# Another order at two joints of a transformer block, and POOL's sums queued behind each other

## The chip, the cores and the metric

The kernel runs on one core of a Trainium2 chip. The metric is the device time of one launch in microseconds (us), the median over the runs shown. A profiled execution comes with it: one launch recorded by the hardware profiler, with the start and length of every instruction of the engines: PE (TensorE's matmuls), PEld (its weight loads), DVE (VectorE), ACT (ScalarE), POOL (GpSimd, here a queue of adding DMAs) and SP (SyncE, here the queue of weight loads).

## The reference, cut to what matters

One block on 512 tokens of width 1024, all in float32:

```
x = x + 0.5 * swiglu(rmsnorm(x), ffn1_w_gu, ffn1_w_down)      # FFN 1, hidden width 2816
x = x + hybrid_mixer(rmsnorm(x), w_in, ..., w_out_conv, w_out_gla, w_o)
x = x + 0.5 * swiglu(rmsnorm(x), ffn2_w_gu, ffn2_w_down)      # FFN 2
return rmsnorm(x)
swiglu(x, w_gu, w_down) = (silu(x @ w_gu[:, :2816]) * (x @ w_gu[:, 2816:])) @ w_down
hybrid_mixer(h, ...)    = (sigmoid(ga) * y_conv + sigmoid(gb) * y_gla) @ w_o
```

`ga`, `gb` and what `y_conv` and `y_gla` are made of are columns of `h @ w_in`; `y_conv` ends in a product with `w_out_conv`, `y_gla` in one with `w_out_gla`.

## The kernel before, in words

**Seven products instead of eight.** Most of the large matrix products are computed by halves of the weight block in both directions (quarters a11, a12, a21, a22), with seven products in place of eight (Strassen-Winograd). Such a group of seven is called a *set*. Its products are named by the weights they use: `m1` (a11), `p2` (a12), `q6` (a11 after a21 has been added to it), `p5` (a21 after a22 has been added to it), `q7` (s3 = a11 + a21, taken before the additions), `p4` (a22), `p3` (a12 after a11 has been added to it).

**Where a product goes.** Each set has three PSUM banks. `m1` opens bank b, from which ACT copies it to bank a; `q6`, `q7` and `p4` are accumulated onto b, `p2` onto a, and `p5` opens c, onto which `p3` is accumulated. Between two products onto bank b the first has to be copied out, or read, by ACT or DVE; the next one cannot start before that.

**Weights.** float32 weights come from HBM by SP's queue (`Weights.dma`, line 349) into ten slots of 512 KB (tiles `f`). The sums among the quarters are DMAs that add, issued on POOL's queue (`Weights.add`, line 376): the *first sum* of a set (a21 += a22), the add of `m1` (a11 += a21) and the add of `p2` (a12 += a11). `s3` is a DVE addition (line 387). Each product's weight is then split into a high part `wh` (a cast on ACT, line 407) and a low part `wl` (a subtraction on DVE, line 408), three buffers of each; the product is wh with the high and the low part of the activations, then wl with the high part. A product with 256-wide matmuls follows the next after 2.88 us.

**The order of the work.** `STEPS` is the list of all products in order, written out by rules: `order` for the sets of `w_gu` ("up sets") and `w_in`, the list `LAST_SEQ` for four sets at the end of the mixer (sets 0 and 1 are `w_out_gla`, 2 and 3 are `w_o`), `wide_sets` for the down products. `Weights.take` hands out the next split weight and issues the work of the steps up to two ahead. `Weights.phase` says at which step a set's loads and its first sum are issued. A scheduler at compile time then fixes each engine's order from the dependencies, the order of the program and its own model of time; on the chip each engine and each queue works through its list in order. `tc.issue_after(ins)` adds a tie: what is issued inside it *on the engine of `ins`* is queued behind `ins`; on other engines it ties nothing.

**The first joint: up sets to down.** In each FFN nine up sets are followed by the two down products. The last up set, here called set 8, is *narrow* (256-wide matmuls, line 566); sets 1 to 7 are wide (line 575). The down product is *lean*: to save slots, its first sum adds a22 straight from HBM onto a21 (`f<-wts` on POOL in the trace), in three pieces, and its products come as `m1` three times, `p5` three times, `q6` three times and so on (line 874).

**The second joint: the end of the mixer.** The operands of the `w_o` sets are made from the outputs of the `w_out_gla` sets, in place, in the order given to `Operands` (`mo`). Their outputs are the new rows of x; when a pair of rows is complete, `NORMS` says where its part of the next RMSNorm is issued (ACT lines 492 to 501, DVE lines 493 and 502).

## Time and profile before

| what | before |
|---|---|
| median of 3 runs (lowest, highest) | 1166.3 us (1165.94, 1167.74) |
| the profiled execution: time; span of its instructions | 1167.14 us; 1165.4 us |
| PE busy, share of the span | 1147.3 us, 98% |
| DVE busy | 994.7 us, 85% |
| ACT busy | 710.0 us, 61% |
| POOL busy | 134.7 us, 12% |
| mean granted TensorE clock | 0.996 |

PE works nearly all the time, so what can be won by order alone is what PE does not work: read first where PE is idle and what ended the wait, then whether the clock was full when it started again. In the views below a row of the timeline gives start, length, engine, line, operation, tiles out<-in, shapes, how many instructions were merged and, in brackets, the idle time before it and what ended that. PE tiles x, y, z, w are the banks of the up sets, `mm` and `aux` those of the others.

### The profile page before, as it was taken

The numbers are of one execution on the slowest core, as the hardware profiler recorded it, in microseconds if no ns is written. First come the engines' busy times: TensorE is split into PE (matmuls) and PEld (weight loads), VectorE is DVE, ScalarE is ACT, GpSimd is POOL, SyncE is SP. The second block draws the span as 40 slices with busy tenths as digits, with TensorE's granted clock in tenths as the row PEclk, the third lists the DMA queues.
The fourth block names the chain that finished last, engine by engine and source line by source line (L and its number), as shares of the span: only waits on it lengthen the run. The fifth ranks groups of instructions, "written<-read, shape, count | busy, mean of one in ns | idle before, by whom it ended". The sixth has DMA issues, their size and how long they took to land. (4 is left out here: it accounts for less than half of the span.)

```text
span 1165.4 us, 17576 instructions
## 1 busy us (share of the span) xinstructions
PE 1147.3 (98%) x6734; PEld 1017.7 (87%) x6734; DVE 994.7 (85%) x1248; ACT 710.0 (61%) x958; POOL 134.7 (12%) x171
## 2 busy tenths in 40 slices
PE   9999999899999999999999999999999999989997
PEld 8898888788888889999989998999889888888886
DVE  7997878779788977979799998699799887888987
ACT  6476666567355655666566586555556666655645
POOL 0011101011020011100101100110001111111100
PEclk9999999999999999999999999999999999999999
DMA  9378787769564488876868867575637878776941
GB/s 354 80 205 201 179 196 178 181 136 255 143 198 134 98 205 232 197 177 172 228 170 210 210 170 216 131 177 150 184 77 199 195 186 183 185 183 138 246 109 73
DMA packets 65764, 208.01 MB, mean 178 GB/s; under 512 B 7216, under 2 KB 13488, under 8 KB 65680
## 3 DMA queue, kind: packets, MB, share of 16 engines
q0 software_dynamic: 21376, 76.03, 35.4%
q1 hardware_dynamic: 39664, 126.37, 32.4%
q10 hardware_dynamic: 4640, 4.49, 1.2%
q8 instruction: 53, 0.87, 0.3%
q14 instruction: 31, 0.25, 0.1%
HBM read 130.32 MB, written 8.39 MB: 119 GB/s over the span
## 5 line engine op out<-in xcount | busy, mean ns | idle before, releaser
L407 ACT CAST wh<-f 128x1024 fp32r<-128x1024 f32 (+1 forms) x366 | 375.6, 1031 | 365.7 <-PE mm L874 41.8
L408 DVE TENSOR_TENSOR wl<-f,wh 128x1024 fp32r<-128x1024 f32 (+1 forms) x366 | 435.9, 1197 | 95.4 <-ACT wh L407 88.7
L376 POOL DMA_DIRECT2D f<-f x132 | 114.7, 871 | 850.4 <-DVE wl L408 545.2
L874 PE MATMUL mm<-wh,op 128*128 128x512 f32 x536 | 133.7, 389 | 0.0
L566 PE MATMUL mm<-op,wh 128*128 128x256 f32 x960 | 127.2, 284 | 0.5 <-ACT op L678 0.4
L566 PEld LDWEIGHTS mm<-op,wh 128*128 128x128 f32 x960 | 120.2, 192 | 1.5 <-ACT op L678 0.6
L874 PEld LDWEIGHTS mm<-wh,op 128*128 128x128 f32 x536 | 100.4, 188 | 20.7
L575 PE MATMUL bb<-op,wh 128*128 128x512 f32 x384 | 97.8, 395 | 0.0
L575 PEld LDWEIGHTS bb<-op,wh 128*128 128x128 f32 x384 | 69.4, 189 | 12.6
L442 PE MATMUL mm<-op,wh 128*128 128x512 f32 x320 | 75.8, 389 | 0.0
L874 PE MATMUL mm<-wl,op 128*128 128x512 f32 x268 | 72.8, 389 | 0.0
L442 PEld LDWEIGHTS mm<-op,wh 128*128 128x128 f32 x320 | 60.0, 188 | 12.5
L566 PE MATMUL mm<-op,wl 128*128 128x256 f32 x480 | 67.8, 283 | 0.0
L575 PE MATMUL z<-op,wh 128*128 128x512 f32 x256 | 64.4, 393 | 0.0
L566 PEld LDWEIGHTS mm<-op,wl 128*128 128x128 f32 x480 | 62.1, 192 | 0.3
L874 PEld LDWEIGHTS mm<-wl,op 128*128 128x128 f32 x268 | 50.3, 188 | 10.5
L575 PEld LDWEIGHTS bb<-op,wl 128*128 128x128 f32 x384 | 52.3, 190 | 5.0 <-DVE wl L408 1.3
L575 PE MATMUL w<-op,wh 128*128 128x512 f32 x224 | 56.3, 393 | 0.0
L575 PE MATMUL bb<-op,wl 128*128 128x256 f32 x384 | 53.6, 282 | 0.9 <-DVE wl L408 0.9
L575 PEld LDWEIGHTS z<-op,wh 128*128 128x128 f32 x256 | 46.0, 189 | 8.3
L779 DVE TENSOR_TENSOR op<-hidw,op 128x1024 fp32r<-128x1024 f32 (+2 forms) x56 | 48.6, 885 | 0.7 <-ACT op L778 0.7
L456 PE MATMUL mm<-op,wh 128*128 128x512 f32 x192 | 48.4, 392 | 0.0
(334 smaller groups left out, 1954.5 us busy)
## 6 DMA issues: line engine op xcount, KB each, us to landing
f<-wts SPq DMA_DIRECT2D x215, 512.0 KB, 4.4
f<-f POOLq DMA_DIRECT2D x128, 512.0 KB, 5.3
f<-wts POOLq DMA_DIRECT2D x10, 512.0 KB, 8.6
f<-wts SPq DMA_DIRECT2D x10, 256.0 KB, 3.5
X<-xT SPq DMA_DIRECT2D x8, 256.0 KB, 4.7
xs<-X POOLq DMA_DIRECT2D x8, 256.0 KB, 3.1
tp<-ga SPq DMA_DIRECT2D x8, 256.0 KB, 5.3
y<-tp SPq DMA_DIRECT2D x7, 256.0 KB, 2.3
```

The lines of the kernel that those rows point to most:

```text
L376: return nc.gpsimd.dma_start(out_, a, accum_op=ALU.add).ins
L407: self.cast = nc.scalar.copy(h[:, :w], raw[:, :w]).ins
L408: nc.vector.tensor_tensor(out=l[:, :w], in0=raw[:, :w], in1=h[:, :w].bitcast(F32), op=ALU.subtract)
L442: nc.tensor.matmul(o, w[:, i * P : (i + 1) * P], a[k], start=j == k == 0, stop=j == 2 and k == kt - 1)
L456: nc.tensor.matmul(o[c], w[:, s : s + P], a[k], start=k == 0 and j == 0, stop=k == kt - 1 and j == 2)
L566: nc.tensor.matmul(o[:, e * HW : (e + 1) * HW], w[:, k * HW + e * P : k * HW + (e + 1) * P], a(k), start=self.fresh and j == k == e == 0, ...
L575: nc.tensor.matmul(o[:, e, :n], w[:, k * HW + e * P : k * HW + (e + 1) * P], a(k), start=self.fresh and k == 0 and w is self.h, stop=k == ...
L779: nc.vector.tensor_tensor(out=l, in0=a, in1=h.bitcast(F32), op=ALU.subtract)
L874: nc.tensor.matmul(o[t], a(k)[:, t * P : (t + 1) * P], ww[:, i * 512 : (i + 1) * 512], start=fresh and j == k == 0, stop=j == 2 and k == s ...
```

## The change

Five edits of order; no arithmetic is added or removed.

1. `order` loses its argument `last`. The last set of a run of sets now ends q6, p5, q7, p2, p4, p3 everywhere. For `w_in` that is what it was; the last up set of each FFN went q6, p2, p5, q7, p4, p3.
2. The first sums of the lean (down) sets are issued two steps ahead of their `m1` instead of three, and are tied with `issue_after` to the last adding DMA issued before (`self.added`, on POOL) instead of to the last cast (`self.cast`, on ACT). The tie of the lean loads on SP to that cast goes.
3. The fourth set of `LAST_SEQ` gets its first sum three steps ahead, as the others, instead of one.
4. `LAST_SEQ`: set 2's `m1` comes ahead of set 1's `p4`; `p5` ahead of `p2` in both `w_o` sets (and in `mo`'s order); the tail of sets 2 and 3 is woven anew.
5. `NORMS`: rows 0 and 1 are normed with rows 2 and 3 after set 3's `q7`, not after set 2's `p3`.

```diff
-def order(firsts, last):
+def order(firsts):
...
+        seq += [(s, "q6"), (s, "p5"), (s, "q7")]
         if i + 1 < n:
             t = firsts[i + 1]
-            seq += [(s, p) for p in ("q6", "p5", "q7")] + [(t, "m1"), (s, "p4")]
+            seq += [(t, "m1"), (s, "p4")]
             seq += [(t, "p2"), (s, "p3")] if i + 2 < n else [(s, "p3")]
         else:
-            seq += [(s, p) for p in last]
+            seq += [(s, "p2"), (s, "p4"), (s, "p3")]
...
 LAST_SEQ = ((0, "m1"), (0, "p2"), (0, "q6"), (0, "p5"), (0, "q7"), (1, "m1"), (0, "p4"),
-            (0, "p3"), (1, "q6"), (1, "p2"), (1, "p5"), (1, "q7"), (1, "p4"), (2, "m1"),
-            (1, "p3"), (2, "p2"), (2, "p5"), (2, "q6"), (3, "m1"), (2, "q7"), (2, "p3"),
-            (2, "p4"), (3, "p5"), (3, "q6"), (3, "p2"), (3, "q7"), (3, "p3"), (3, "p4"))
-LAST = ("q6", "p2", "p5", "q7", "p4", "p3")
+            (0, "p3"), (1, "q6"), (1, "p2"), (1, "p5"), (1, "q7"), (2, "m1"), (1, "p4"),
+            (1, "p3"), (2, "p5"), (2, "p2"), (2, "q6"), (3, "m1"), (3, "p5"), (2, "q7"),
+            (3, "p2"), (2, "p4"), (3, "q6"), (2, "p3"), (3, "q7"), (3, "p3"), (3, "p4"))
...
-    last = ("q6", "p5", "q7", "p2", "p4", "p3") if mats == "w_in" else LAST
...
-                    ahead = 1 if (PLAN[n][0], STEPS[i - 1][1]) == ("w_o", "q6") else 3
-                    self.sums.setdefault(max(lo + 3, i - ahead), []).append(n)
+                    self.sums.setdefault(max(lo + 3, i - (2 if lean(n) else 3)), []).append(n)
...
-            with tc.issue_after(self.cast) if lean(n) else ExitStack():
-                nc.sync.dma_start(t[:, :w], self.block(n))
+            nc.sync.dma_start(t[:, :w], self.block(n))
...
-                return nc.gpsimd.dma_start(out_, a, accum_op=ALU.add).ins
+                self.added = nc.gpsimd.dma_start(out_, a, accum_op=ALU.add).ins
+                return self.added
...
-                self.first[n] = (self.add(a21[:, :w], self.block(n + 3), self.cast) if lean(n)
+                self.first[n] = (self.add(a21[:, :w], self.block(n + 3), self.added) if lean(n)
                                  else self.add(a21, a22))
...
-            ("m1", "p2", "p5", "q6", "q7", "p3", "p4"))
+            ("m1", "p5", "p2", "q6", "q7", "p3", "p4"))
...
-        NORMS = {(0, "p3"): (0, 1), (1, "q7"): (2, 3), (1, "p4"): range(4, KD)}
+        NORMS = {(1, "q7"): range(4), (1, "p4"): range(4, KD)}
```

## The prediction

> **What bounds the kernel now.** I read the page first, then who PE waited for, then PE's timeline around each of those waits.

> ```profile
> PE 1147.3 (98%) x6734; PEld 1017.7 (87%) x6734; DVE 994.7 (85%) x1248; ACT 710.0 (61%) x958; POOL 134.7 (12%) x171
> PE y L566 <- ACT tp L745: 6.6, 2, 3.3
> PE y L566 <- ACT x L732: 1.4, 1, 1.4
> ```

> PE bounds it, with 18.1 us of the span not busy. The waits (engine, tile and line, what ended them, total, times, longest) are few: 3.3 us twice and 1.4 us once on the bank y of an up set (three rows left out are waits at the start, for a wl, and one that follows below). Where are they, and what do they cost? PE's timeline, FFN 1:

> ```profile
> 204.50 2.00 PE L575 MATMUL z<-op,wh 128*128 128x512 f32 x8
> 207.29 2.00 PE L575 MATMUL w<-op,wh 128*128 128x512 f32 x8
> 211.67 2.18 PE L566 MATMUL y<-op,wh 128*128 128x256 f32 x16 [1.43 <-ACT x L732]
> 214.64 2.08 PE L566 MATMUL x<-op,wh 128*128 128x256 f32 x16
> 217.52 2.08 PE L566 MATMUL z<-op,wh 128*128 128x256 f32 x16
> 220.40 2.08 PE L566 MATMUL y<-op,wh 128*128 128x256 f32 x16
> 226.78 3.27 PE L566 MATMUL y<-op,wh 128*128 128x256 f32 x16 [3.34 <-ACT tp L745]
> 234.12 2.00 PE L874 MATMUL mm<-wh,op 128*128 128x512 f32 x8
> ```

> The first two rows are set 7's last products, the last row is the down product. Between them run set 8's last six products, in the order q6, p2, p5, q7, p4, p3, on the banks y, x, z, y, y, z (p3 is not shown). q7 and p4 follow each other on one bank, and there PE waits 3.34 us. What follows is slow too: p4's 16 matmuls take 3.27 us where q7's took 2.08. Another product of one length starts 2.88 us later (214.64, 217.52, 220.40), after a wide one the next starts 2.79 us later (204.50, 207.29), so q6 was due at 210.08 and down at 210.08 + 6 x 2.88 = 227.36. It came at 234.12: **6.8 us lost**. FFN 2:

> ```profile
> 1030.74 2.08 PE L566 MATMUL y<-op,wh 128*128 128x256 f32 x16
> 1045.64 3.00 PE L566 MATMUL y<-op,wh 128*128 128x256 f32 x16 [3.22 <-ACT tp L745]
> 1052.98 2.00 PE L874 MATMUL mm<-wh,op 128*128 128x512 f32 x8
> ```

> Here q6 came on time, and down was due at 1030.74 + 17.28 = 1048.02: **5.0 us lost**. The stretches of the clock (length, busy time of the engines, then PE's clock, DMA share, GB/s):

> ```profile
> core 0: us, PE busy (x) PEld busy (x) DVE busy (x) ACT busy (x) POOL busy (x), PEclk, DMA share, GB/s
> 210.30:211.60 1.30, 0.00 (x0) 0.00 (x0) 1.30 (x2) 1.30 (x3) 0.00 (x0) 1.00 0.70 137
> 226.80:230.20 3.40, 3.40 (x18) 3.40 (x19) 3.10 (x4) 1.25 (x3) 0.86 (x1) 0.59 0.35 94
> 1045.70:1049.00 3.30, 3.30 (x19) 3.30 (x20) 3.06 (x4) 1.42 (x3) 0.87 (x1) 0.64 0.42 112
> ```

> After waits of 3.34 and 3.22 us PE ran at a granted clock of 0.59 and 0.64 over some 3.4 us, which costs 1.7 us more or so; after the 1.43 us wait it kept 1.00. [...]

> Now the second joint. Twenty-eight products of 2.88 us start at 740.98 and should end at 821.62; the next stage starts at 823.23:

> ```profile
> 740.98 2.08 PE L566 MATMUL mm<-op,wh 128*128 128x256 f32 x16
> 796.63 3.19 PE L566 MATMUL mm<-op,wh 128*128 128x256 f32 x24 [0.39 <-ACT op L678]
> 816.09 2.94 ACT L407 CAST wh<-f 128x1024 fp32r<-128x1024 f32 x3 [3.90 <-DMA f<-f]
> 823.23 2.00 PE L456 MATMUL mm<-op,wh 128*128 128x512 f32 x8
> ```

> **1.6 us lost** in all, 0.39 of it in a wait for q7's operand, some more where ACT's cast for set 3's p3 waited 3.90 us for the add of p2, which is only two products ahead of p3.

> **Part 1, set 8's p2 moves behind q7.** The products are the same; only the order changes. What held p4 in FFN 1:

> ```profile
> 222.67 1.49 DVE L845 SCALAR_TENSOR_TENSOR hidw<-hidw 128x1280 f32<-128x1280 f32 x1
> 224.25 1.04 ACT L778 CAST op<-hidw 128x1024 fp32r<-128x1024 f32 x1 [1.66 <-DVE hidw L845]
> 225.20 1.04 ACT L407 CAST wh<-f 128x1024 fp32r<-128x1024 f32 x1
> 226.15 0.58 ACT L745 COPY tp<-y 128x512 f32<-128x512 f32 x1
> ```

> ACT had q7's copy (L745) behind a cast of a down operand, itself waiting for DVE, and a weight cast. The copy ended at 226.73, q7 at 226.78 - 3.34 = 223.44: 3.29 us. With p2 on bank x between q7 and p4, 2.88 us of that lie beside PE's work, if ACT keeps that order, and 0.4 us is left. FFN 2 has a wait of 3.22, so 0.3 us is left. Both are far below the 1.43 us after which the clock held, so its loss goes as well.

> The price: q6 and q7 have one product (p5) between them instead of two. q6's copy:

> ```profile
> 218.09 0.57 ACT L745 COPY tp<-y 128x512 f32<-128x512 f32 x1
> ```

> It ended at 218.66; q6 was over when p2 began, at 214.64 or a little after, so some 3.9 us, 1.0 us more than p5 covers. I take 0 for it, since in every other up set q6, p5, q7 stand just so and the list of PE's waits has no third wait on a copy; 1.0 us for each FFN stays as the bound. The second price: p2's add (a12 += a11) has to land before p3's cast, and now only p4 lies between p2 and p3. p2's wh takes the buffer that q6's frees after its 16 matmuls of 24, 1.9 us; with a cast (1.05), wl (1.23) and the issue, the add goes out about 4.6 us after q6's start.

> The page's row of POOL's adds (KB each, median us to landing) and the landing times of line 376:

> ```profile
> f<-f POOLq DMA_DIRECT2D x128, 512.0 KB, 5.3
> DMA to landing us min/median/max: 3.2/5.3/12.1
> ```

> With the median of 5.3 us it lands at 9.9; p3 is due at 5 x 2.88 = 14.4 and its cast takes 1.05, so 3.4 us are to spare: nothing lost. At the longest landing, 12.1 us, p3 is 3.4 us late. [...]

> **Part 2, the down sums wait their turn on POOL.** In FFN 1, with the down product's second and fourth piece last:

> ```profile
> 196.40 1.23 DVE L408 TENSOR_TENSOR wl<-f,wh 128x1024 fp32r<-128x1024 f32 x1 [0.54 <-ACT wh L407]
> 199.22 0.86 POOL L376 DMA_DIRECT2D f<-wts  x1 [13.59 <-DVE tp L750]
> 199.80 1.16 POOL L376 DMA_DIRECT2D f<-f  x1
> 200.34 1.52 POOL L376 DMA_DIRECT2D f<-wts  x1
> 209.14 1.05 ACT L407 CAST wh<-f 128x1024 fp32r<-128x1024 f32 x1 [6.21 <-DMA f<-f]
> 214.15 0.86 POOL L376 DMA_DIRECT2D f<-f  x1 [1.47 <-DVE wl L408]
> 236.87 1.98 PE L874 MATMUL mm<-wh,op 128*128 128x512 f32 x8
> 240.95 1.98 PE L874 MATMUL mm<-wh,op 128*128 128x512 f32 x8
> ```

> m1's wl of set 8 ended at 197.63; its add (f<-f) went at 199.80, behind a down sum (f<-wts) that held the queue until 199.22, and landed when the cast of q6 could start, at 209.14: 9.3 us after issue, two down sums beside it. That made the 1.43 us wait ahead of q6. The old tie, to a cast on ACT, held nothing on POOL: the second down sum went at 200.34, before the cast of set 8's q6. The new one does: all three go behind p2's add (214.15 here, about 214.7 after). m1's add then goes at about 197.9 and lands by 203 with the median; q6 is on time, 1.4 us less.

> The cost is on the down side. Queued behind each other, a second add took 9.3 us against 5.3, so I space landings by 4.5 us: p2's at 220, the sums' at 224.5, 229, 233.5. The first readers are the three p5 pieces of down: the first started 6.8 us after down (240.95 against 234.12), and a piece takes 2.7 (236.87), so they are due at 227.36 + 6.8, 9.5 and 12.3 us; with a cast each they have 8.6, 6.9 and 5.1 us to spare. The bounds are 0 and, with p2's add at 12.1 us, 1.7 us in each FFN. I take 0. The second half of down starts 7 x 6.8 = 48 us after the first, which leaves its sums ample time behind the same queue. The loads on SP lose a tie that tied nothing there: 0.

> So FFN 1 wins 6.8 - 0.4 = 6.4 us, FFN 2 5.0 - 0.3 = 4.7 us. Does PE's earlier arrival last? DVE and ACT must keep up:

> ```profile
> 205.00:228.00 23.00, 18.24 (x135) 17.25 (x134) 17.58 (x20) 14.60 (x20) 1.73 (x2) 0.99 0.78 190
> 234.00:260.00 26.00, 26.00 (x118) 21.53 (x117) 20.13 (x24) 17.78 (x25) 5.14 (x6) 1.00 0.68 142
> ```

> DVE (third) is idle for 5.4 us in the first stretch and 5.9 in the second: what it does before down fits, and a rest of it finds room after.

> **Parts 3 to 5, the `w_o` sets.** At most the 1.6 us come back. p2 of set 3 moves ahead to five products before its p3, so the 3.90 us wait of ACT goes; set 3's p5 between q6 and q7 of set 2 covers the 0.39. Against that, rows 0 and 1 are normed later: a quarter of the norm's work on ACT and DVE moves into the last three products, and set 1's p4 comes one product later with its long chain to p2's operand:

> ```profile
> 780.00:800.00 20.00, 19.61 (x162) 19.35 (x161) 19.33 (x26) 11.91 (x18) 1.72 (x2) 1.00 0.74 181
> ```

> With 0.7 us of DVE idle in 20, what comes late there is not caught up; I bound the loss by two waits like the one of 0.39 us, one for each moved chain. Between +0.8 and -1.6 I take -0.4, the wait that stands in the list. The first sum of set 3, issued earlier, cannot run before its loads: 0.

> **Sum.** 6.4 + 4.7 + 0.4 = 11.5 us. The profiled execution took 1167.14 us (span 1165.4 and 1.7 around it), 0.8 above the median: it gives 1155.6, and against the median **1154.8 us**. Its own range: both q6 copies late and a loss at `w_o` is 1154.8 + 2.0 + 1.2 = 1158.0; no rest at all and the whole 1.6 is 1154.8 - 0.7 - 1.2 = 1152.9.

> **Rivals.**
> (a) A long wait stays in one FFN. ACT's order is made anew at compile time; the down operands' casts and DVE work (L845) may be put ahead of another copy, and a wait above 3.2 us brings the slow clock with it. For it: ACT idled 1.66 us behind L845 in the middle of the joint. Against: `w_in`'s last set has the same order and no wait. One such wait is 4.9 us: 1159.7.
> (b) p3 waits for p2's add. If it lands after 12.1 us in both FFNs, p3 is 3.4 us late, and with 1.7 of clock that is 10.2: 1165.0, no change. For it: 9.3 us were seen with two transfers beside it. Against: it is now first in its queue, the sums behind it.
> (c) The other side, slower: the down sums arrive too late. From 5.1 us of delay on PE waits, and from there on each FFN pays the rest and, above 3.2 us, 1.7 for the clock; the 11.5 us won are gone at a delay of 9.2 us, and the kernel is slower by more than 0.2% from 10.3 on. At 11 us each FFN loses 5.9 + 1.7 = 7.6: 1154.8 + 15.2 = 1170.0. For it: POOL's queue is in order, and one late add holds all three. Against: POOL is busy for 12% of the span, and the longest landing seen is 6.8 us above the median.
> (d) The tie changes nothing, or the scheduler had these orders anyway: then only the reordering counts, and 1.4 us less is won: 1156.2, inside the first range.

> **How the numbers follow.** The forecast with (d) has 0.63, (a) 0.17, (b) 0.08, (c) 0.08; 0.04 is for better than 1152.5. The range from 1152.5 to 1162.0 holds the forecast's range and most of (a), 0.8. No change means within 0.2%, 2.3 us, about what a measurement of this kernel can tell: above 1164.0 it is no gain. Faster 0.84 (forecast, (a), better), same 0.08, slower 0.08.

> **What would show it.** In the profile after: PE's wait on ACT L745 gone or under 0.6 us, no granted clock below 1.00 in either joint; down starting 17.3 to 18.3 us after q6; in POOL's rows two f<-f before the first f<-wts of each FFN; ACT's cast of q6 no longer waiting for a DMA; no ACT cast behind `f<-wts` at p5 of down; 80.6 to 82.0 us from the first product of `w_out_gla` to FFN 2. Wrong would be a new PE row on wl or wh ahead of p3, or ahead of down's p5, above 3 us.

## The result, and the profile after

| | before | after |
|---|---|---|
| median (lowest to highest), runs of one job | 1166.12 us (1164.48 to 1167.74), 4 runs | 1156.99 us (1156.81 to 1157.24), 4 runs |
| ratio after / before, 95% interval | | 0.9922 [0.9905, 0.9939] |
| the profiled execution; its span | 1167.14 us; 1165.4 us | 1156.81 us; 1155.0 us |

Faster by 9.1 us; the forecast was 1154.8 us, 2.2 less than measured. Lines of the changed kernel carry numbers four or five lower (L745 is L741, L407 is L403, L376 is L371, L874 is L870, L845 is L841). First the row of PE on the page after, and PE's waits:

```profile
PE 1143.9 (99%) x6734; PEld 1014.2 (88%) x6734; DVE 994.1 (86%) x1248; ACT 709.8 (61%) x958; POOL 134.7 (12%) x171
...
PE mm L562 <- ACT op L674: 0.7, 1, 0.7
PE mm L870 <- DVE hidw L1010: 0.4, 2, 0.2
PE y L562 <- ACT tp L741: 0.2, 1, 0.2
```

The two waits of 3.3 us on q7's copy and the one of 1.4 us ahead of q6 are gone; 0.15 us is left of them. PE does the same 6734 matmuls in 3.4 us less of busy time: 3.0 of that are the two stretches of half clock (from p4 to down 7.34 us before in both FFNs, 5.86 and 5.85 after). PE's timeline after, first FFN 1, then FFN 2 (set 8 in the order q6, p5, q7, p2, p4, p3; the last rows are down):

```profile
207.18 2.00 PE L571 MATMUL w<-op,wh 128*128 128x512 f32 x8
209.97 2.08 PE L562 MATMUL y<-op,wh 128*128 128x256 f32 x16
215.73 2.08 PE L562 MATMUL y<-op,wh 128*128 128x256 f32 x16
218.61 2.08 PE L562 MATMUL x<-op,wh 128*128 128x256 f32 x16
221.80 2.18 PE L562 MATMUL y<-op,wh 128*128 128x256 f32 x16 [0.15 <-ACT tp L741]
227.66 0.39 PE L870 MATMUL mm<-wh,op 128*128 128x512 f32 x1
228.27 1.88 PE L870 MATMUL mm<-wh,op 128*128 128x512 f32 x7 [0.22 <-DVE hidw L1010]
...
230.89 1.98 PE L870 MATMUL mm<-wh,op 128*128 128x512 f32 x8
...
1024.53 2.08 PE L562 MATMUL y<-op,wh 128*128 128x256 f32 x16
1042.07 0.39 PE L870 MATMUL mm<-wh,op 128*128 128x512 f32 x1
```

q6 starts when it is due (207.18 + 2.79 = 209.97). Down starts 17.69 and 17.54 us after q6, where six products of 2.88 make 17.28: 0.4 and 0.3 us are lost at the two joints of up sets and down (one in each FFN) in place of 6.8 and 5.0. The stretches with the clock (PE busy first, PEclk third from the end):

```profile
205.00:228.00 23.00, 22.85 (x176) 21.80 (x174) 19.94 (x23) 15.44 (x23) 4.39 (x5) 1.00 0.67 157
```

In the same window before, PE was busy for 18.24 us of 23 and the clock was 0.99. POOL's queue and three rows of ACT in FFN 1, after:

```profile
197.81 0.86 POOL L371 DMA_DIRECT2D f<-f  x1 [12.29 <-DVE wl L404]
214.69 0.86 POOL L371 DMA_DIRECT2D f<-f  x1 [16.03 <-DVE wl L404]
215.23 2.99 POOL L371 DMA_DIRECT2D f<-wts  x3
...
203.63 1.05 ACT L403 CAST wh<-f 128x1024 fp32r<-128x1024 f32 x1 [0.81 <-PE y L562]
220.22 1.05 ACT L403 CAST wh<-f 128x1024 fp32r<-128x1024 f32 x1 [3.56 <-DMA f<-f]
221.18 0.57 ACT L741 COPY tp<-y 128x512 f32<-128x512 f32 x1
```

m1's add goes out at 197.81, when its wl is done, and not behind a down sum; the cast of q6 on ACT starts at 203.63 and waits for PE to free a buffer, no longer for a DMA; before it started at 209.14. These 5.5 us turn out to be the heart of the matter.

By stages of the profiled executions: 6.3 and 4.7 us are won at these two joints and 0.5 in the `w_o` stage (81.78 us against 82.25), of which 0.3 is lost again at the start of FFN 2 (from the first product of the stage to one of FFN 2's first up products, 740.98 to 893.48 before and 734.98 to 887.28 after, it is 152.50 and 152.30 us). And 0.5 is given back in each down product (107.00 against 106.52 us, 105.40 against 104.91). There the second matmul of down waits, because its bank is the one that p4 used: DVE's read of it (L1010) stands behind a subtraction for a down operand (L841). The list has this wait at 0.22 us, but matmuls overlap (one takes 0.39 us, eight take 2.00), and it is all of the 0.5: from the first product of down to the second it is 3.23 us (227.66 to 230.89), before 2.75 (234.12 to 236.87).

### The profile page after: what moved, and what is told of

It is laid out like the page before. It is cut to its first block, busy times and chain, and to the rows that moved or that the text cites. A ratio compares the mean times of both kernels' runs of the same rounds, so it can differ in the third digit from the quotient of the medians.

```text
span 1155.0 us, 17571 instructions
## 1 busy us (share of the span) xinstructions
PE 1143.9 (99%) x6734; PEld 1014.2 (88%) x6734; DVE 994.1 (86%) x1248; ACT 709.8 (61%) x958; POOL 134.7 (12%) x171
## 4 chain that ended last, share of the span: by engine, by line
PE 94%; DVE 2%; ACT 1%; issue 1%; DMA 1%; POOL 0%; ACTq 0%; DVEq 0%; POOLq 0%
PE mm L870 16%; PE mm L562 14%; PE bb L571 11%; PE mm L438 9%; PE z L571 8%; PE w L571 7%; PE y L571 6%; PE mm L452 6%; PE aux L870 6%; PE x L571 3%; PE y L562 2%; PE w L562 2%; PE aux L562 1%; DVE wl L404 1%; PE x L562 1%
## 5 line engine op out<-in xcount | busy, mean ns | idle before, releaser
L403 ACT CAST wh<-f 128x1024 fp32r<-128x1024 f32 (+1 forms) x366 | 375.9, 1031 | 361.3 <-PE mm L562 47.9
L371 POOL DMA_DIRECT2D f<-f x132 | 114.0, 864 | 911.9 <-DVE wl L404 609.4
L870 PE MATMUL mm<-wh,op 128*128 128x512 f32 x536 | 134.2, 390 | 0.4 <-DVE hidw L1010 0.4
L870 PEld LDWEIGHTS mm<-wh,op 128*128 128x128 f32 x536 | 100.4, 188 | 21.7 <-DVE hidw L1010 1.1
L870 PE MATMUL mm<-wl,op 128*128 128x512 f32 x268 | 72.8, 389 | 0.0
L870 PEld LDWEIGHTS mm<-wl,op 128*128 128x128 f32 x268 | 50.3, 188 | 10.4
## 6 DMA issues: line engine op xcount, KB each, us to landing
f<-wts SPq DMA_DIRECT2D x215, 512.0 KB, 4.4
f<-f POOLq DMA_DIRECT2D x128, 512.0 KB, 5.2
f<-wts POOLq DMA_DIRECT2D x10, 512.0 KB, 9.0
```

The source lines that it names most:

```text
L371: self.added = nc.gpsimd.dma_start(out_, a, accum_op=ALU.add).ins
L403: self.cast = nc.scalar.copy(h[:, :w], raw[:, :w]).ins
L870: nc.tensor.matmul(o[t], a(k)[:, t * P : (t + 1) * P], ww[:, i * 512 : (i + 1) * 512], start=fresh and j == k == 0, stop=j == 2 and k == s ...
```

## The experiments

The forecast put nearly all of the gain down to the order (part 1) and 1.4 us to the tie (part 2). The first four runs take the parts singly.

**e1: the order of the up sets alone.**

```
-LAST = ("q6", "p2", "p5", "q7", "p4", "p3")
+LAST = ("q6", "p5", "q7", "p2", "p4", "p3")
```

> The kernel before, with only the last up set's order changed to q6, p5, q7, p2, p4, p3; the down sums stay where they were in POOL's queue. Theory A (two causes that add: the bank shared by q7 and p4, and POOL's order ahead of q6): the two waits of 3.3 us and their slow clock go, 9 to 10 us less, about 1157; the 1.4 us wait ahead of q6 in FFN 1 stays. Theory B (the tie on POOL is what pays: with p2 one product ahead of p3, its add must not stand behind a down sum): p3 or p4 waits about 3 us in each FFN and most of the gain is lost, 1161 to 1166.

1163.81 us (1161.87 to 1165.98, 12 runs), ratio 0.9976 [0.9967, 0.9984]: 2.6 us, not the bulk, and inside theory B's range. PE's waits, and the cast of q6 on ACT in FFN 1:

```profile
PE y L566 <- ACT tp L745: 4.9, 4, 1.9
PE y L566 <- ACT x L732: 1.8, 2, 1.7
...
209.40 1.05 ACT L407 CAST wh<-f 128x1024 fp32r<-128x1024 f32 x1 [6.47 <-PE w L575]
```

The two long waits have become six shorter ones (ahead of q6, q7 and p4), because everything on ACT is still as late as before: the cast of q6 starts at 209.40, 5.8 us later than in the changed kernel. (The row puts the idle time down to PE; but POOL still sends a down sum, at 199.54, ahead of m1's add, at 200.12, and that add landed at 209.30, 0.1 us ahead of the cast.) In FFN 2 the clock fell once more (0.50 from 1045.74 to 1049.15); there q7's copy, at 1043.81, stands behind p3's cast, which waited 3.84 us for p2's add, as in rival (b). Between the time at which q6 is due and down 4.4 and 5.3 us are lost, against 6.8 and 5.0 before.

**e2: the tie of the down sums alone** (part 2, with the old order, in which q7 and p4 stand side by side on one bank).

```
-ahead = 1 if (PLAN[n][0], STEPS[i - 1][1]) == ("w_o", "q6") else 3
+ahead = 1 if (PLAN[n][0], STEPS[i - 1][1]) == ("w_o", "q6") else 2 if lean(n) else 3
...
-self.first[n] = (self.add(a21[:, :w], self.block(n + 3), self.cast) if lean(n)
+self.first[n] = (self.add(a21[:, :w], self.block(n + 3), self.added) if lean(n)
```

> The kernel before, with only the down sums' tie to the last adding DMA and their two steps ahead; the up order is the old one (q7 and p4 next to each other). Theory A: m1's add goes about 1.4 us earlier and lands in 5 us instead of 9, so the 1.4 us wait ahead of q6 in FFN 1 goes and nothing else: 1.4 us less, about 1164.7; both 3.3 us waits stay with their slow clock. Theory B: the waits shrink too, 1160 to 1162.

1158.19 us (1157.66 to 1158.45, 5 runs), ratio 0.9928 [0.9916, 0.9940]: 8.2 us, nearly the whole gain and more than either theory had. PE's wait, POOL, and ACT at q6's cast, set 7's copy, a Silu and q7's copy:

```profile
PE y L566 <- ACT tp L745: 1.8, 2, 1.1
...
198.17 0.85 POOL L375 DMA_DIRECT2D f<-f  x1 [12.30 <-DVE wl L408]
209.38 0.85 POOL L375 DMA_DIRECT2D f<-f  x1 [10.36 <-DVE wl L408]
...
203.98 1.05 ACT L407 CAST wh<-f 128x1024 fp32r<-128x1024 f32 x1 [0.81 <-PE y L566]
207.73 0.59 ACT L765 COPY tp<-z 128x512 f32<-128x512 f32 x1
213.40 0.63 ACT L1019 ACTIVATE tp<-tp 128x512 f32<-128x512 f32 x1
222.45 0.58 ACT L745 COPY tp<-y 128x512 f32<-128x512 f32 x1
```

The same instructions in the kernel before:

```profile
212.50 0.58 ACT L765 COPY tp<-z 128x512 f32<-128x512 f32 x1
217.55 0.63 ACT L1019 ACTIVATE tp<-tp 128x512 f32<-128x512 f32 x1 [2.58 <-DVE tp L758]
```

With q6's cast 5.2 us earlier (203.98 for 209.14), set 7's copy, which stands behind it in ACT's order, is 4.8 us earlier, the Silu 4.2, and q7's copy 3.7 (222.45 for 226.15). PE's wait on that copy is 1.07 us instead of 3.34, with the two products still side by side, and with every instruction of PE, ACT and DVE in the order of the kernel before.

**e3: the `w_o` part alone** (parts 3 to 5).

> The kernel before, with only the w_o part (order of the last four sets, order of the operands, norms of rows 0 and 1, first sum of set 3). Theory A: 0.5 us less, as in the stage's length in the trace after (81.8 us against 82.3). Rival: the stage is set by DVE, which is 97% busy there, and what is won is given back behind it: 0.

1165.79 us (1163.35 to 1167.87, 11 runs), ratio 0.9997 [0.9988, 1.0006]: nothing that can be told from zero. Its own stage took 81.79 us for 82.25, the same 0.46 us as in the changed kernel, but by the up product at 891.98, 152.31 us after the first of the stage, 0.19 of it is left, as in the changed kernel. So the rival has more than half of it, and the spread of the runs hides the rest.

**e4: the wait filled with work.** The kernel before, with twelve matmuls of ones on bank x between q7 and p4, so that p4 is as late as ever but PE not idle.

```
 if p == "q7":
     s.onto("c", s.q7)
+    if i == (KF - plain) // 2 - 1:
+        o = MM2("x")[:, 0]
+        for _ in range(12):
+            nc.tensor.matmul(o[:, :P], ones, ones, start=True, stop=True)
```

> The kernel before, with twelve matmuls of ones (128 wide, into the free bank x, read by nothing) put between the last up set's q7 and p4 in both FFNs, where PE idles 3.3 us. The wait for q7's copy stays. Theory A (the wait and the slow clock behind it are two prices): PE is not idle long enough any more, the clock stays at 1.00 and p4 takes 2.1 us instead of 3.0 to 3.3: 1.7 us less in each FFN, about 1162.8, and the spread of the runs narrows. Rival (p4 is slow for another cause, its operands or weights): no change, 1166.

1163.20 us (1162.41 to 1166.01, 6 runs), ratio 0.9977 [0.9966, 0.9988]. The clock held through both joints (0.998 in the mean of the execution, 0.996 before) and p4 ran at its usual pace:

```profile
225.14 2.18 PE L566 MATMUL y<-op,wh 128*128 128x256 f32 x16 [0.64 <-ACT tp L745]
...
230.99 1.32 PE L874 MATMUL mm<-wh,op 128*128 128x512 f32 x5
```

Wait and slow clock are two prices. From p4 to down it is 5.85 us here and 7.34 before (226.78 to 234.12), and FFN 2 has 5.84 and 7.34: the slow clock costs 1.5 us each time, where the forecast had 1.7. The difference of the times, 3.2 us, holds something else too: in this execution q6 came on time. In those of e3 and e13, whose code for FFN 1 is that of before up to q7, q6 is 0.2 us late at most, so the wait of 1.4 us ahead of it comes and goes from run to run. The runs spread over 3.6 us; that the spread narrows, as expected, is not shown.

These runs left the forecast's account of part 1 and part 2 standing the wrong way round. New theory: m1's add, held behind a down sum on POOL, made ACT late by 5 us, and the copy of q7 inherited it. Rivals: m1's add costs the 1.4 us ahead of q6 alone; or it is p2's add that gains, with the down sums now behind it.

**e5: the down sums behind m1's add only.** The tie of e2, but with `self.added` set by the adds of `m1` alone; on POOL one pair trades places in each FFN, the third down sum still goes ahead of p2's add, and the orders of PE, ACT, DVE and SP are those of the kernel before, instruction by instruction. Its lines carry numbers one lower.

```
-self.add(a11[:, :w], a21[:, :w], self.first[twin])
+self.added = self.add(a11[:, :w], a21[:, :w], self.first[twin])
```

> The old orders, and the down sums held behind the last up set's m1 add alone: on POOL the first of them trades places with that add, the third still stands ahead of p2's add, and nothing moves on PE, DVE or ACT. Theory (a late m1 add was what made both joints late: it held the cast of q6 on ACT for 6.2 and 4.4 us, and through ACT's and DVE's order the copy of q7): m1's add goes at about 198.2 and lands by 204, no granted clock below 1.00, waits on the copies of at most 1.2 us, and nearly all of the tie's gain, 1158 to 1160 us. Rival A (my prediction's step: m1's add is worth the wait of 1.4 us ahead of q6 and no more): 1164 to 1165 us, with a wait of over 3 us still between q7 and p4. Rival B (the gain comes from p2's add, now free of the sums beside it): 1162 to 1165 us, p2's add landing near 219.5 as before.

1158.72 us (1158.17 to 1160.35, 5 runs), ratio 0.9937 [0.9924, 0.9951]: 8.0 us by one swap on one queue in each FFN. POOL, q6's cast, p3's cast and q7's copy, and PE's wait:

```profile
198.04 0.85 POOL L375 DMA_DIRECT2D f<-f  x1 [12.30 <-DVE wl L407]
199.20 0.86 POOL L375 DMA_DIRECT2D f<-wts  x1 [0.30 <-DMA f<-wts]
...
203.85 1.05 ACT L406 CAST wh<-f 128x1024 fp32r<-128x1024 f32 x1 [0.81 <-PE y L565]
220.49 1.05 ACT L406 CAST wh<-f 128x1024 fp32r<-128x1024 f32 x1 [3.12 <-DMA f<-f]
223.33 0.58 ACT L744 COPY tp<-y 128x512 f32<-128x512 f32 x1
...
PE y L565 <- ACT tp L744: 2.9, 2, 2.1
```

Theory held, both rivals fell as the main cause. One number missed: I expected waits of at most 1.2 us, and FFN 1 has one of 2.08. There p2's add, sent at 212.80 behind the third down sum, holds ACT for 3.12 us at p3's cast, and q7's copy comes 0.9 us later than in e2: the second rival's mechanism, with that much of the time. FFN 2's wait is 0.81 us.

**e10: the changed kernel without its `w_o` part** (the order and the tie together).

> The changed kernel without its w_o part: both FFN joints as there. If the reordering of the up sets still brings something on top of the tie, it stands between the tie alone (1158.2) and the changed kernel (1157.0), at the latter plus what the w_o stage won in the trace, 0.5 us: 1157.3 to 1157.6. Rival: with m1's add on time the order makes no difference, and the 1.2 us between those two came from the w_o stage: 1158.0 to 1158.4.

1157.67 us (1156.97 to 1159.48, 5 runs), ratio 0.9928 [0.9916, 0.9941]. It lies where the order adds some 0.5 us to the tie and the `w_o` part 0.7, but its runs reach over both forecasts: unclear by the times. The trace has PE's loss at the joints at 0.6 and 0.0 us, against 1.3 and 1.0 in e2, so the order adds some 1.7 us there. But e10's down products take 0.5 us longer each (107.02 and 105.44 against 106.51 and 104.91 in e2), since the wait for p4's bank comes with the order: 0.7 us of the 1.7 are left.

Three waits were left in the changed kernel. Each can be taken away by one more tie.

**e9: the `w_o` wait.** The scheduler had put the first matmuls of set 2's q7 ahead of set 3's p5, and their operand (L674) came last. The tie puts q7 behind the last matmul issued before it on PE, here p5's (`W.last` is set in the loop of the matmuls, not shown):

```
...
-Product(*W.take(), self.group.get(p), fresh).narrow(self.bank[n])
+f = Product(*W.take(), self.group.get(p), fresh)
+with tc.issue_after(W.last) if p == "q7" else ExitStack():
+    f.narrow(self.bank[n])
```

> The changed kernel with the PE tie of the w_o stage alone: set 2's q7 behind set 3's p5. Its wait of 0.70 us there goes, the stage takes 81.1 us instead of 81.8, and the kernel 1156.2 to 1156.5. Rival: q7's operand is needed right behind p5 either way, and PE waits for it there instead: 1156.9.

1156.38 us (1155.98 to 1156.74, 4 runs), ratio 0.9916 [0.9902, 0.9929]. The wait in the changed kernel, and in e9 the first row of the stage and of the next:

```profile
790.75 2.65 PE L562 MATMUL mm<-op,wh 128*128 128x256 f32 x20 [0.70 <-ACT op L674]
...
735.80 2.08 PE L562 MATMUL mm<-op,wh 128*128 128x256 f32 x16
816.64 1.55 PE L452 MATMUL mm<-op,wh 128*128 128x512 f32 x6
```

The stage takes 80.84 us, 0.94 less than in the changed kernel and 0.2 above 28 products of 2.88: nothing took the wait's place.

**e8: that tie and two more.** On ACT, p3's cast behind q7's copy; on DVE, the subtraction for down's q6 behind p4's read of its bank:

```
...
+with tc.issue_after(self.held) if p == "p3" and self.held else ExitStack():
     self.cast = nc.scalar.copy(h[:, :w], raw[:, :w]).ins
...
 if p == "q6":
-    self.minus(b(1, 1), b(0, 1))
+    with tc.issue_after(W.behind):
+        self.minus(b(1, 1), b(0, 1))
```

> The changed kernel with three ties more: on ACT q7's copy ahead of p3's cast, on DVE the subtraction for down's q6 behind p4's read of its bank, on PE set 2's q7 behind set 3's p5 in the w_o stage. The waits that the trace of the changed kernel has left at these places are 0.15, two of 0.22 and 0.70 us. If each goes and nothing takes its place, 1.3 us less than the changed kernel: 1155.5 to 1156.0. Rival: the subtraction, later now, makes an operand of down late, and part of it comes back as a wait inside down: 1156.5 to 1158.

1156.61 us (1156.19 to 1156.95, 4 runs), ratio 0.9918 [0.9904, 0.9931]: the rival. Nothing is lost at either joint any more, but the tie gave DVE and ACT another order behind it in FFN 2, and inside the down product there PE waits for weights (lines L879 and L405 are L870 and L403 of the changed kernel):

```profile
1068.05 2.11 PE L879 MATMUL mm<-wh,op 128*128 128x512 f32 x8 [0.27 <-ACT wh L405]
1071.76 1.42 PE L879 MATMUL mm<-wh,op 128*128 128x512 f32 x5 [0.70 <-ACT wh L405]
```

The cast ahead of the first of these waits starts at 1066.94, in e11, without the tie there, at 1064.95.

**e11: the same with DVE's tie in FFN 1 alone.**

> The three ties of e8, the one for down's q6 in FFN 1 alone: in e8 it won 0.27 us ahead of down there and, in FFN 2, pushed casts into down, where PE then waited 0.27 and 0.70 us for wh. Expected: down of FFN 2 takes 105.4 us again instead of 106.5, and the kernel 1155.4 to 1156.0, the fastest of the set. Rival: what FFN 1 wins ahead of down is given back within it, and the time is that of e9, 1156.4.

1155.15 us (1154.66 to 1155.50, 4 runs), ratio 0.9908 [0.9892, 0.9925]: the fastest of the set and a little under the expected range, 1.8 us under the changed kernel by the medians of different jobs, though the intervals of the two ratios overlap. FFN 2's down takes 104.9 us, 0.5 less than expected, and no joint of up sets and down loses anything.

**e12 and e13: behind which waits the clock fell.** e5 had kept its clock after a wait of 2.08 us, e1 had lost it after one of 1.86. The fill of e4 with 5 and with 6 matmuls leaves waits of about 2 us.

> The kernel before with 5 matmuls of ones, some 1.2 us, put into each wait between q7 and p4, so that PE is idle there for some 2.0 to 2.2 us at a stretch. Two theories of the slow clock. By steps: the clock changes on a grid of 3.413 us counted from the start of its full speed, and falls for one step after a step in which PE was busy for less than about 1.6 us (1.55 dropped it, 1.72 did not, in the runs so far); whether it falls here depends on where the wait lies in the grid, and the traces must agree with that, wait for wait. By length: it falls after a wait above some threshold, which the runs so far contradict (1.86 us dropped it, 2.08 us did not). Time 1162 to 1166 us, no forecast between the two.

> The same with 6 matmuls of ones, some 1.4 us: stretches of idle PE of some 1.8 to 2.0 us. By steps of the grid: the clock falls for one step of 3.413 us only behind a step with less than about 1.6 us of busy PE, which 1.8 us of idleness inside one step reaches and the same idleness across two steps does not. By length: both waits of a run do the same. Time 1162 to 1166 us.

1167.43 and 1162.77 us, a single execution of each; the first lies above the expected range, with both clock drops and the wait ahead of q6. In the trace of the kernel before the record of the full clock starts at 5.57 us, and the clock is at 0.50 for 3.413 us from 227.44 and from 1046.63 on, which is 65 and 305 times 3.413 us later, to 0.1 us. So the rows below cut the time into steps of 3.413 us, counted from the start of the full clock; in each pair of rows the step with the wait and the one behind it (PE busy first, PEclk third from the end). Before, FFN 1; e1, FFN 1 and FFN 2; e5, FFN 1; e12, FFN 1; e13, FFN 2:

```profile
224.03:227.44 3.41, 0.66 (x5) 0.66 (x6) 3.41 (x4) 3.19 (x5) 0.00 (x0) 1.00 0.64 207
227.44:230.85 3.41, 3.41 (x18) 3.41 (x17) 2.46 (x4) 1.25 (x2) 0.86 (x1) 0.50 0.42 81
...
209.48:212.89 3.41, 1.73 (x15) 1.52 (x14) 2.37 (x3) 3.41 (x5) 0.86 (x1) 1.00 0.64 133
212.89:216.30 3.41, 3.41 (x31) 3.41 (x30) 3.38 (x5) 2.34 (x3) 0.00 (x0) 1.00 0.80 144
1042.33:1045.74 3.41, 1.55 (x14) 1.35 (x13) 1.32 (x2) 2.88 (x4) 0.00 (x0) 1.00 0.51 161
1045.74:1049.15 3.41, 3.41 (x19) 3.41 (x18) 3.41 (x5) 3.22 (x5) 0.34 (x1) 0.50 0.49 149
...
220.16:223.57 3.41, 1.72 (x15) 1.51 (x13) 2.17 (x3) 3.08 (x4) 0.00 (x0) 1.00 0.59 197
223.57:226.99 3.42, 3.03 (x25) 3.03 (x26) 3.42 (x5) 2.36 (x4) 0.86 (x1) 1.00 0.84 334
...
224.01:227.42 3.41, 1.20 (x10) 1.01 (x9) 3.41 (x4) 3.10 (x5) 0.00 (x0) 1.00 0.56 189
227.42:230.83 3.41, 3.41 (x19) 3.41 (x17) 2.55 (x4) 1.21 (x2) 0.86 (x1) 0.50 0.41 81
...
1040.15:1043.56 3.41, 1.75 (x16) 1.56 (x15) 3.41 (x3) 3.36 (x5) 0.00 (x0) 1.00 0.83 276
1043.56:1046.97 3.41, 3.41 (x31) 3.41 (x30) 3.41 (x6) 1.73 (x3) 0.87 (x1) 1.00 0.52 105
```

Steps with 0.66, 1.20 and 1.55 us of busy PE are followed by a step at half clock, steps with 1.72, 1.73 and 1.75 are not. In the kernel before one more step, 1043.22 to 1046.63, has as little (0.99 us) and half clock behind it; all others there and in the changed kernel, up to the end of PE's work, have 2.03 us or more, and none has half clock behind it. By length the waits don't sort: e13's other wait, 1.99 us in FFN 1, lay across two steps (2.50 and 2.33 us busy) and cost no clock; e12's of 2.06 in FFN 2 lay within one (1.35 us busy) and did.

## Why the prediction was right, and where it was not

Right by its number and its signs, but for a wrong reason in the larger part. The sum was bounded by what PE lost at the joints, and since the two parts were changed together, it came out whichever of them was the cause: that is luck, not understanding.

- **Losses at the joints (6.8 and 5.0 us).** They were there to be won: 0.4 and 0.3 remain, the rests that the forecast named. Their agreement is partly chance: in FFN 1 the copy of q7 is no longer late for the reason in the forecast's rows, but because p3's cast, ahead of it on ACT, waits 3.56 us for p2's add. That is rival (b)'s mechanism, at a few tenths of a microsecond.
- **Part 1, what held p4: the step that failed.** The forecast read ACT's rows ahead of q7's copy, found a cast waiting for DVE (L845), and stopped there. It did not ask why DVE and ACT were late. e5 answers: swap one pair on POOL and most of the wait goes, with the orders of PE, ACT and DVE left alone. The order, credited with 9.7 us (6.4 + 4.7 less the 1.4 of the tie), brings 2.6 by itself, and on top of the tie 1.7 us at the joints, of which 1.0 is lost again in down.
- **Part 2, the tie: mis-sized.** Its mechanism was right down to the times (m1's add at 197.9 forecast, 197.81 measured; the cast of q6 without a DMA wait), its price was read off PE's wait ahead of q6 alone: 1.4 us, where the tie alone measured 8.2 (e2) and its m1 half 8.0 (e5). PE had hidden all but 1.4 us of a delay of 5 at q6; ACT and DVE had not, and handed it on to the next thing PE needed from them, q7's copy, 13 us later. Rival (d), that the tie changes nothing, fell.
- **The costs set at nothing.** q6's copy, with one product less to hide behind: nothing (213.58, well ahead of q7 at 215.73). Down sums behind p2's add: no cast of a down operand waited for one of them at the first p5. But down gave back 0.5 us in each FFN, 1.0 of the 2.2 us by which the forecast was too low: the wait for p4's bank at down's second matmul, which the forecast did not look for.
- **The clock.** Its price (1.7 us a time) was nearly right, e4 shows 1.5. Its condition, a wait above some 3 us, was not: the clock fell behind waits of 1.86 us (e1) and 2.06 us (e12).
- **Parts 3 to 5.** -0.4 forecast, -0.47 in the stage, -0.2 with what is lost behind it; as a time it can't be told from zero (e3). The agreement is luck. The forecast took the wait for q7's operand, 0.39 us, as what goes; it grew to 0.70 (L674, e9). What was won lies elsewhere, 0.5 us of it in the last three products (808.12 to 816.76, 814.06 to 823.23 before), where p3's cast no longer waits 3.90 us for p2's add, the half of its reasoning that held.
- **The base.** The profiled execution of before stood 1.0 us above the median of its job, that of after 0.2 below: of the 10.4 us between the two spans 9.1 remain between the medians.

## What to carry to other kernels

Follow a late instruction back past the first engine that was busy: where its queue was late as a whole, find the first wait of that queue, here a cast on ACT 17 us ahead of the copy that PE waited for, held by POOL's queue. A small wait of the bounding engine can be the visible tip of a large delay on the others, so price a removed wait by how late the *helpers* become, not by PE's share of it. And a tie added to remove one wait moves others: try it at one place at a time (e8 against e11).
